# The down projections of both FFNs by seven block products over 16 of their 22 weight rows

## The chip, the cores and the metric

The kernel runs on one core of one Trainium2 chip. The metric is device time in microseconds of one execution; lower is better. The core's engines work side by side, each through its own queue in order: TensorE (PE; its weight loads are listed as PEld) multiplies, VectorE (DVE) and ScalarE (ACT) do elementwise work, GpSimd (POOL) a little of it, and SyncE (SP) issues the transfers between main memory and SBUF.

## The reference

Two layers on 512 tokens of width 1024, float32. Layer 0 mixes tokens with an RWKV-7 recurrence, layer 1 with a gated spatial unit; each is followed by a dense SwiGLU FFN with hidden width 2816, and each sub-layer sits between two RMSNorms.

```python
def _swiglu(x, w_gate, w_up, w_down):
    return (jax.nn.silu(x @ w_gate) * (x @ w_up)) @ w_down

for i in range(DEPTH):                                  # DEPTH = 2
    ...                                                 # token mixer i
    h = _rmsnorm(x, norm_gains[i, 2])
    h = _swiglu(h, ffn_w_gate[i], ffn_w_up[i], ffn_w_down[i])   # (512,1024) -> (512,1024)
    x = x + _rmsnorm(h, norm_gains[i, 3])
```

The change touches only the last product of `_swiglu`: activations of 512 tokens by 2816 times `w_down` of 2816 by 1024.

## The kernel before

**Precision.** Every float32 operand is split into two parts of type fp32r: `split` (L178) has ACT cast the tile to `hi` (L179) and DVE compute the remainder `lo` (L180). `mm3` (L201) then issues three matmuls, hi x hi, hi x lo and lo x hi (L204), into one PSUM bank. So a weight tile of 128 x 2 x 512 costs a load, a cast of 1024 columns on ACT and a remainder of 1024 columns on DVE; a row of activations costs 512 columns on each.

**Gate and up.** `ffn` (L366) makes the activations in 11 pairs of 128-row blocks. The first `PLAIN` pairs (3 in layer 0, 2 in layer 1) run directly. The others, up to pair 10, run as seven block products each, steps `p1` to `p7` (L403 to L464): two token halves of 256, two halves of the 1024 inputs, gate and up weights side by side. A step has 24 matmuls 128x128 by 128x256. Weight sums `wsum` are made by DVE (L398). PSUM banks R, Q and Z collect the products; DVE and ACT combine them (`cc<-Q` at L450, `cc<-Z` at L457, the gates at L421 and L423). Weight splits go to four rotating pairs of tiles, two in pool `wp` and two in `wx`, so that at most four are held ahead of PE.

**Down.** `out_proj` (L285) multiplies the 22 activation rows, split lazily by `down` (L503) into tiles `actw`, with `w_down`. A weight unit is two rows of 128 by one half (512) of the columns, loaded to `wraw` by SP and split by `weight` (L182). `first(0)` runs the 11 units of the first column half into four banks `acc`, one for each block of 128 tokens, unit by unit. `post0` (L316) then squares each block for its norm on ACT and multiplies it by the gain on DVE, while `first(1)` runs the second half's first eight units into four other banks. The last three units of the second half (`tail=3`) are run block by block instead, and each finished block is normalised and added to x by `post1` (L326) while PE works on the next. In layer 0 the norm of the next sub-layer follows block by block; in layer 1 each block is stored.

**Slots.** SBUF tiles of one size come from two rotating sets, 13 slots "x" and 17 slots "s". The 11 activation pairs sit in "s".

**The order.** The program is written in the order above; a scheduler then sets the order of each engine's instructions by its own model of times, and puts in the semaphores. An instruction at the head of an engine's queue holds up all behind it.

Of the kernel before, what the change touches and what calls it, by code (L numbers as in the profile page):

```python
# [7 lines left out]
F32 = mybir.dt.float32  # L8
F32R = mybir.dt.float32r
I32 = mybir.dt.int32  # L10
AF = mybir.ActivationFunctionType
ALU = mybir.AluOpType

P = 128
T = 512
# [7 lines left out]
NJ = DFF // P  # L23
# [13 lines left out]
XSLOTS = 13  # L37
LAG = 2
PLAIN = (3, 2)
DECAY = 0.5 * 0.6065306597126334  # L40


# [43 lines left out]
class Quads:  # L86
# [22 lines left out]
    def first(self):  # L109
        self.b11 = self.raw(0, 0)  # L110
        self.split(1, self.b11, "s")
        self.b21 = self.raw(1, 0)
        self.split(2, self.b21, "s")
# [17 lines left out]
class Trunk:  # L131
# [150 lines left out]
    def prenorm(self, col):  # L282
        return Norm(self, col)

    def out_proj(self, acts, wrows, nk, row, xts, store=None, tail=3, norm=None, spare=None, mid=None, after=()):  # L285


        nc = self.nc
        v = nc.vector
        gain = self.bcast_row(row)  # L290
        nu = nk // 2
        cols = [slice(0, 512), slice(512, 1024)]
        late = (1, 1) if spare else (0, tail)
        accs, f0, part = [None, None], [], []

        def mms(half, k, tt, w):
            tok = slice(tt * P, (tt + 1) * P)
            hi, lo = acts(k)
            self.mm3(accs[half][tt], (hi[:, tok], lo[:, tok]), w, k == 0, k == nk - 1)

        def unit(half, u):
            own = spare if half and u < nu - late[1] else None
# [4 lines left out]
            return [(2 * u + j, (hi[:, j, :], lo[:, j, :])) for j in range(2)]  # L307

        def first(half):
            accs[half] = self.accs(half)  # L310
            for u in range(nu - late[half]):
                for k, w in unit(half, u):
                    for tt in range(TT):
                        mms(half, k, tt, w)
# [21 lines left out]
                nc.sync.dma_start(out=store[tt * P:(tt + 1) * P, :], in_=xts[tt])  # L336

        hn_tile = lambda: self.sm.tile([P, D], F32, name="hn", tag="hn", bufs=2)
        first(0)
        if not spare:  # L340
            for tt in range(TT):
                post0(tt, hn_tile()[:, 0:512])
# [4 lines left out]
        for tt in range(TT):  # L347
# [5 lines left out]
            hn = hn_tile()  # L353
# [12 lines left out]
    def ffn(self, li, xts, norm, store=None, nxt=None, early=()):  # L366
        nc = self.nc
        early = list(early)
        v, a = nc.vector, nc.scalar
        gains = self.i["norm_gains"]  # L370
        wgu = self.gate_up(li)
        first = PLAIN[li]
        wd = self.i["ffn_w_down"][li].rearrange("(u j p) n -> u p j n", p=P, j=2)
        hT, b = norm.hT, {}
        acts, pairs, loads, seeded = [], {}, [0], []
# [123 lines left out]
                p(n)  # L499

        halves = {}

        def down(k):  # L503
            if k not in halves:
                t = halves[k] = self.slot([P, 2, T], F32R, "actw", "x" if k < XSLOTS else "s")
                self.split(t[:, 0], t[:, 1], acts[k // 2][:, k % 2])
            return halves[k][:, 0], halves[k][:, 1]

        self.out_proj(down, lambda u: wd[u], NJ, gains[li, 3], xts, store, norm=nxt)


    def load_features(self):
# [793 lines left out]
```

## Time and profile before

| | us |
|---|---|
| median of three runs | 1335.92 (1330.71 to 1341.78) |
| the profiled execution | 1336.29 |
| its span, first to last instruction | 1334.6 |
| mean granted TensorE clock | 0.981 |
| FFN 0: gate and up, about | 461 to 693 |
| FFN 0: down, about | 693 to 815 |
| FFN 1: gate and up, about | 970 to 1198 |
| FFN 1: down, about | 1198 to 1328 |

The span is the profiled execution's time less 1.7 us around it. A group's row reads: line, engine, operation, tile written <- tiles read, shapes, xcount | busy us, mean ns of one | idle time of the engine before them and what ended it. A timeline row reads: start, length, engine, line, operation, shapes, and in brackets the idle time before it with what ended it. A few records of matmuls can be missing from a trace, so a stretch may count some less than were issued.

### The profile page before, as it was taken

What the parts mean: (1) busy time and instruction counts of PE and PEld (TensorE: products, weight loads), DVE (VectorE), ACT (ScalarE), POOL (GpSimd) and SP (SyncE); (2) the same over time, 40 slices, a digit from 0 to 9 for tenths busy, and PEclk for the clock granted to TensorE, in tenths of its full rate; (3) what the DMA queues carried; (4) which work ended last, traced back from release to release, by engine and by line L of the source; (5) the groups of instructions that cost most, each with busy time, mean ns of one, the idle gap of its engine ahead of it and who ended that gap; (6) DMA issues with size and microseconds to landing.
All of it is one profiled execution on the core that took longest, in us unless ns stands there. A gap on an engine that the chain in (4) does not pass through costs nothing.

```text
span 1334.6 us, 24342 instructions
## 1 busy us (share of the span) xinstructions
PE 1281.5 (96%) x9740; PEld 1112.1 (83%) x9740; DVE 885.4 (66%) x1481; ACT 690.0 (52%) x1237; POOL 160.7 (12%) x304
## 2 busy tenths in 40 slices
PE   5999999989989899999999999999999999999998
PEld 3677799878867698999998887878888999998886
DVE  6975856567946787877874326476679878785223
ACT  7976884676533454444563315443464445464221
POOL 0000383666000012000000003020002000000000
PEclk9999999999889999999999999999989999999999
DMA  5137694322243215433423332343430443323231
GB/s 160 41 101 178 154 212 132 98 64 80 69 124 117 79 56 151 111 99 108 127 64 116 111 95 74 111 142 95 126 96 11 117 127 96 100 75 126 95 95 64
DMA packets 217202, 140.10 MB, mean 105 GB/s; under 512 B 67792, under 2 KB 193280, under 8 KB 217088
## 3 DMA queue, kind: packets, MB, share of 16 engines
q1 hardware_dynamic: 215792, 133.81, 34.9%
q0 software_dynamic: 1296, 4.72, 1.1%
q8 instruction: 77, 1.26, 0.4%
q14 instruction: 37, 0.30, 0.1%
HBM read 124.35 MB, written 14.16 MB: 104 GB/s over the span
## 4 chain that ended last, share of the span: by engine, by line
PE 66%; DVE 6%; ACT 2%; DMA 2%; issue 2%; POOL 1%; SPq 0%; DVEq 0%; ACTq 0%; POOLq 0%
PE acc L204 27%; PE Q L204 10%; PE gu L204 9%; PE R L204 7%; PE Z L204 7%; PE u L204 3%; DVE wlo L180 1%; PE gh L993 1%; DMA wraw<-in_rwkv_w_o_dram 1%; ACT hn L249 1%; ACT whi L179 1%; PE s L1240 1%; DVE wsum L400 0%; DVE tm L923 0%; ACT hT L60 0%
## 5 line engine op out<-in xcount | busy, mean ns | idle before, releaser
L180 DVE TENSOR_TENSOR wlo<-wraw,whi 128x1024 fp32r<-128x1024 f32 x117 | 144.9, 1238 | 194.8 <-ACT whi L179 194.3
L179 ACT CAST whi<-wraw 128x1024 fp32r<-128x1024 f32 x117 | 122.6, 1049 | 236.1 <-PE acc L204 143.1
L204 PE MATMUL acc<-whi,actw 128*128 128x512 f32 x704 | 220.7, 394 | 0.0
L204 PEld LDWEIGHTS acc<-whi,actw 128*128 128x128 f32 x704 | 132.2, 188 | 30.6
L204 PE MATMUL Q<-bc,whi 128*128 128x256 f32 x816 | 147.4, 281 | 2.2 <-ACT hn L444 2.2
L204 PE MATMUL acc<-wlo,actw 128*128 128x512 f32 x352 | 138.5, 394 | 0.0
L204 PEld LDWEIGHTS Q<-bc,whi 128*128 128x128 f32 x816 | 125.6, 189 | 2.7 <-ACT hn L444 2.6
L204 PE MATMUL gu<-hT,whi 128*128 128x256 f32 (+1 forms) x448 | 112.8, 344 | 2.3 <-ACT hT L60 1.2
L204 PE MATMUL Q<-bc,wlo 128*128 128x256 f32 x408 | 114.6, 281 | 0.0
L179 ACT CAST whi<-wsum 128x1024 fp32r<-128x1024 f32 x68 | 71.1, 1052 | 81.2 <-PE Q L204 24.3
L204 PE MATMUL Z<-bc,whi 128*128 128x256 f32 x544 | 99.6, 281 | 0.0
L204 PE MATMUL R<-bc,whi 128*128 128x256 f32 x544 | 98.9, 281 | 0.0
L180 DVE TENSOR_TENSOR wlo<-wsum,whi 128x1024 fp32r<-128x1024 f32 x68 | 82.2, 1221 | 22.6 <-ACT whi L179 21.6
L204 PEld LDWEIGHTS gu<-hT,whi 128*128 128x128 f32 x448 | 79.4, 199 | 12.6 <-ACT hT L60 1.9
L179 ACT CAST whi<-wq 128x1024 fp32r<-128x1024 f32 x51 | 53.5, 1049 | 68.4 <-PE gu L204 20.9
L204 PEld LDWEIGHTS Z<-bc,whi 128*128 128x128 f32 x544 | 84.0, 189 | 0.0
L204 PEld LDWEIGHTS R<-bc,whi 128*128 128x128 f32 x544 | 83.8, 188 | 0.2
L204 PE MATMUL proj<-xsp,whi 128*128 128x512 f32 x256 | 82.5, 401 | 1.3 <-ACT r L687 1.3
L180 DVE TENSOR_TENSOR wlo<-wq,whi 128x1024 fp32r<-128x1024 f32 x51 | 65.3, 1284 | 22.8 <-ACT whi L179 22.6
L204 PEld LDWEIGHTS acc<-wlo,actw 128*128 128x128 f32 x352 | 66.1, 188 | 15.1
L204 PEld LDWEIGHTS Q<-bc,wlo 128*128 128x128 f32 x408 | 77.2, 189 | 0.0
L204 PE MATMUL R<-bc,wlo 128*128 128x256 f32 x272 | 76.5, 281 | 0.0
(352 smaller groups left out, 2839.9 us busy)
## 6 DMA issues: line engine op xcount, KB each, us to landing
wraw<-in_ffn_w_down_dram SPq DMA_DIRECT2D x44, 512.0 KB, 3.7
wq<-in_ffn_w_gate_dram SPq DMA_DIRECT2D x68, 256.0 KB
wq<-in_ffn_w_up_dram SPq DMA_DIRECT2D x68, 256.0 KB, 4.3
wraw<-in_rwkv_w_rkv_dram SPq DMA_DIRECT2D x24, 512.0 KB, 5.4
wraw<-in_sgu_w_in_dram SPq DMA_DIRECT2D x16, 512.0 KB, 3.8
wraw<-in_ffn_w_gate_dram SPq DMA_DIRECT2D x10, 512.0 KB
wraw<-in_ffn_w_up_dram SPq DMA_DIRECT2D x10, 512.0 KB, 3.9
x<-in_x_dram SPq DMA_DIRECT2D x8, 512.0 KB, 3.3
```

What stands on the lines that cost most here:

```text
L179: self.nc.scalar.copy(hi, src)
L180: self.nc.vector.tensor_tensor(lo, src, hi.bitcast(F32), op=ALU.subtract)
L204: self.nc.tensor.matmul(out, l, r, start=start, stop=stop, skip_group_check=resumed)
L249: self.nc.scalar.activation(junk, src, AF.Square, accum_out=s)
L993: mm(gh[:, cc * P:(cc + 1) * P], mt[rows, cc, :], bx[rows, 0:2, cc, :], start=True, stop=True)
L1240: mm(acc[:, tt * P:(tt + 1) * P], vt[tt][:, m * P:(m + 1) * P], wsT[:, m, :], start=True, stop=True)
```

## The change

With `CROSS = (4, 4)`, each layer's down projection splits its rows: units 0 to 7 (16 rows of 128) are done by seven block products, units 8, 9 and 10 (six rows) plainly as before. `s = 4`: units 0 to 3 are the near half of the inner dimension, 4 to 7 the far half. The tokens are split into `g` (first 256) and `u` (last 256), the 1024 columns into two halves. A product `q1` to `q7` runs over four units; each unit multiplies a 256-token block of activations (split into `ablk`) by a 128 x 2 x 512 tile of weights, in 12 matmuls 128x128 by 128x512.

The eight banks have names: `R` (two banks) is the first column half of the first 256 tokens, `V` that of the last 256, `Z` and `Q` the second half of the same tokens. Each product adds into one of these pairs; where a product belongs to several outputs, ACT copies the bank to `t0` or `t1` and DVE adds the copy into another bank. `tb` and `ta` (tiles `tsum`) hold weight sums and are changed in place from step to step, `sums` (tiles `asum`) activation sums. Five of the seven products load weights, 20 loads in all, into tiles `wc` that alternate between the two buffers of `wraw` and the two of `f0`, or straight into `ta`.

The written order is p, q1, p, q5, p, q6, q2, q3, q7, q4, where each p is one plain unit's first column half into R and V. `out_proj` then gets the banks as `begun`: it does not run `first(0)`, calls `post0` for the four blocks after q4, has nothing left for `first(1)`, and runs the tail of the second half as before.

On VectorE, in layer 0, at the end of gate/up (`cc<-Q` of pair 10 up to its last product's sum `act<-cc`), before:

```order
L450 SCALAR_TENSOR_TENSOR cc<-Q,hn 128x512
L457 TENSOR_TENSOR cc<-Z,hn 128x512
L180 TENSOR_TENSOR wlo<-wraw,whi 128x1024
L180 TENSOR_TENSOR actw<-act,actw 128x512 x9
L180 TENSOR_TENSOR wlo<-wraw,whi 128x1024
L180 TENSOR_TENSOR actw<-act,actw 128x512 x2
L459 TENSOR_TENSOR act<-cc 128x2x256
```

and after, at the same place:

```order
L455 SCALAR_TENSOR_TENSOR cc<-Q,hn 128x512
L182 TENSOR_TENSOR wlo<-wc,whi 128x1024
L521 TENSOR_TENSOR tsum<-tsum,wc 128x1024
L182 TENSOR_TENSOR actw<-act,actw 128x512
L462 TENSOR_TENSOR cc<-Z,hn 128x512
L182 TENSOR_TENSOR ablk<-act,ablk 128x512 x4
L521 TENSOR_TENSOR tsum<-tsum,wc 128x1024
L577 TENSOR_TENSOR asum<-act 128x512 x2
L521 TENSOR_TENSOR asum<-act 128x512 x2
L182 TENSOR_TENSOR wlo<-wc,whi 128x1024
L182 TENSOR_TENSOR actw<-act,actw 128x512
L464 TENSOR_TENSOR act<-cc 128x2x256
```

The eleven activation splits are replaced by two of them, four block splits, two weight sums and four activation sums (L577 for q5, L521 for q7); the first `wlo<-wc` is that of q1's first unit, the second that of its second unit.

On TensorE, in layer 0, before, the change from the first column half (`acc_8091`, `acc_8092` are its last two blocks) to the second (`acc_8524` and on):

```order
L204 MATMUL acc_8091<-whi_8455,actw_8474 128x512
L204 MATMUL acc_8092<-whi_8455,actw_8474 128x512
L204 MATMUL acc_8092<-wlo_8456,actw_8474 128x512
L204 MATMUL acc_8092<-whi_8455,actw_8474 128x512
L204 MATMUL acc_8524<-whi_8530,actw_8099 128x512
L204 MATMUL acc_8524<-wlo_8531,actw_8099 128x512
```

and after, the change from q7 (`acc_8093`, `acc_8094` are Q) to q4 (`acc_8089` is V's first bank):

```order
L206 MATMUL acc_8093<-whi_8735,ablk_8732 128x512
L206 MATMUL acc_8094<-whi_8735,ablk_8732 128x512
L206 MATMUL acc_8094<-wlo_8736,ablk_8732 128x512
L206 MATMUL acc_8094<-whi_8735,ablk_8732 128x512
L206 MATMUL acc_8089<-whi_8760,ablk_8757 128x512
L206 MATMUL acc_8089<-wlo_8761,ablk_8757 128x512
```

Before, the next banks needed nothing from the last ones; now the first matmul of q4 comes after an addition of Q's copy into `acc_8089`. On VectorE that addition stands behind the one into the same Q bank:

```order
L622 TENSOR_TENSOR acc_8093<-acc_8093,hn_8107 128x512
L623 TENSOR_TENSOR acc_8089<-acc_8089,hn_8108 128x512
L622 TENSOR_TENSOR acc_8094<-acc_8094,hn_8107 128x512
L623 TENSOR_TENSOR acc_8090<-acc_8090,hn_8108 128x512
L182 TENSOR_TENSOR wlo_8818<-tsum_8106,whi_8817 128x1024
```

The last row is the weight remainder of the fourth unit of q4. The four additions stood nowhere in the program before.

```diff
@@ -37,6 +37,8 @@
 XSLOTS = 13
 LAG = 2
 PLAIN = (3, 2)
+CROSS = (4, 4)
+CROSS_ORDER = ("p1p5p62374", "p1p5p62374")
 DECAY = 0.5 * 0.6065306597126334
 
 
@@ -282,7 +284,7 @@
     def prenorm(self, col):
         return Norm(self, col)
 
-    def out_proj(self, acts, wrows, nk, row, xts, store=None, tail=3, norm=None, spare=None, mid=None, after=()):
+    def out_proj(self, acts, wrows, nk, row, xts, store=None, tail=3, norm=None, spare=None, mid=None, after=(), begun=None):
 
 
         nc = self.nc
@@ -291,12 +293,13 @@
         nu = nk // 2
         cols = [slice(0, 512), slice(512, 1024)]
         late = (1, 1) if spare else (0, tail)
-        accs, f0, part = [None, None], [], []
+        u0, accs = begun if begun else (0, [None, None])
+        f0, part = [], []
 
         def mms(half, k, tt, w):
             tok = slice(tt * P, (tt + 1) * P)
             hi, lo = acts(k)
-            self.mm3(accs[half][tt], (hi[:, tok], lo[:, tok]), w, k == 0, k == nk - 1)
+            self.mm3(accs[half][tt], (hi[:, tok], lo[:, tok]), w, k == 0, k == nk - 1, u0 > 0)
 
         def unit(half, u):
             own = spare if half and u < nu - late[1] else None
@@ -307,8 +310,9 @@
             return [(2 * u + j, (hi[:, j, :], lo[:, j, :])) for j in range(2)]
 
         def first(half):
-            accs[half] = self.accs(half)
-            for u in range(nu - late[half]):
+            if not u0:
+                accs[half] = self.accs(half)
+            for u in range(u0, nu - late[half]):
                 for k, w in unit(half, u):
                     for tt in range(TT):
                         mms(half, k, tt, w)
@@ -336,7 +340,8 @@
                 nc.sync.dma_start(out=store[tt * P:(tt + 1) * P, :], in_=xts[tt])
 
         hn_tile = lambda: self.sm.tile([P, D], F32, name="hn", tag="hn", bufs=2)
-        first(0)
+        if not begun:
+            first(0)
         if not spare:
             for tt in range(TT):
                 post0(tt, hn_tile()[:, 0:512])
@@ -499,14 +504,135 @@
                 p(n)
 
         halves = {}
+        s = CROSS[li]
 
         def down(k):
             if k not in halves:
-                t = halves[k] = self.slot([P, 2, T], F32R, "actw", "x" if k < XSLOTS else "s")
+                t = halves[k] = self.slot([P, 2, T], F32R, "actw", "x" if k - 4 * s < XSLOTS - 3 * s else "s")
                 self.split(t[:, 0], t[:, 1], acts[k // 2][:, k % 2])
             return halves[k][:, 0], halves[k][:, 1]
 
-        self.out_proj(down, lambda u: wd[u], NJ, gains[li, 3], xts, store, norm=nxt)
+        def cross():
+            accs = [self.accs(0), self.accs(1)]
+            R, V, Z, Q = accs[0][0:2], accs[0][2:4], accs[1][0:2], accs[1][2:4]
+            near = range(s)
+            act = lambda n, tok: acts[n][:, :, tok]
+            cols = (slice(0, 512), slice(512, 1024))
+            sub = lambda o, x, y: v.tensor_tensor(o, x, y, op=ALU.subtract)
+            sums = [self.slot([P, 2, 2, 256], F32, "asum", "x") for _ in near]
+            ta, tb = ([self.slot([P, 2, 512], F32, "tsum", "x") for _ in near] for _ in range(2))
+            t0, t1 = (self.sm.tile([P, 2, 512], F32, name="hn", tag="hn", bufs=2) for _ in range(2))
+            rest = list(range(2 * s, NJ // 2))
+
+            def load(n, half, t=None):
+                if t is None:
+                    pool, tag = ((self.wp, "wraw"), (self.f0p, "f0"))[loads[0] % 2]
+                    loads[0] += 1
+                    t = pool.tile([P, 2, 512], F32, name="wc", tag=tag, bufs=2)
+                nc.sync.dma_start(out=t, in_=wd[n][:, :, cols[half]])
+                return t
+
+            def parts(w):
+                self.nw += 1
+                wp = self.wx if self.nw % 2 else self.wp
+                hi, lo = (wp.tile([P, 2, 512], F32R, name=t, tag=t, bufs=2) for t in ("whi", "wlo"))
+                self.split(hi, lo, w)
+                return hi, lo
+
+            def product(ps, left, right, start=False):
+                for p in near:
+                    x, w = left(p), right(p)
+                    at = self.slot([P, 2, 2, 256], F32R, "ablk")
+                    self.split(at[:, 0], at[:, 1], x)
+                    hi, lo = parts(w)
+                    for j in range(2):
+                        for m in range(2):
+                            tok = slice(m * P, (m + 1) * P)
+                            self.mm3(ps[m], (at[:, 0, j, tok], at[:, 1, j, tok]), (hi[:, j], lo[:, j]),
+                                     start and p == 0 and j == 0, p == s - 1 and j == 1, True)
+
+            def straight():
+                n = rest.pop(0)
+                hi, lo = parts(load(n, 0))
+                for j in range(2):
+                    ah, al = down(2 * n + j)
+                    for m, q in enumerate(R + V):
+                        tok = slice(m * P, (m + 1) * P)
+                        self.mm3(q, (ah[:, tok], al[:, tok]), (hi[:, j], lo[:, j]), n == 2 * s and j == 0,
+                                 not rest and j == 1, True)
+
+            def q1():
+                def w(p):
+                    t = load(p, 0)
+                    load(p, 1, ta[p])
+                    sub(tb[p], ta[p], t)
+                    return t
+                product(Q, lambda p: act(p, g), w, True)
+                for m in range(2):
+                    a.copy(t1[:, m], Q[m])
+                    v.tensor_tensor(R[m], R[m], t1[:, m], op=ALU.add)
+
+            def q5():
+                def x(p):
+                    v.tensor_tensor(sums[p][:, 0], act(p, u), act(s + p, u), op=ALU.add)
+                    return sums[p][:, 0]
+                product(Z, x, lambda p: tb[p], True)
+                for m in range(2):
+                    a.copy(t0[:, m], Z[m])
+
+            def q6():
+                def x(p):
+                    sub(sums[p][:, 0], sums[p][:, 0], act(p, g))
+                    return sums[p][:, 0]
+
+                def w(p):
+                    sub(tb[p], load(s + p, 1), tb[p])
+                    return tb[p]
+                product(Q, x, w)
+                for m in range(2):
+                    a.copy(t1[:, m], Q[m])
+
+            def q2():
+                def w(p):
+                    t = load(s + p, 0)
+                    sub(tb[p], t, tb[p])
+                    return t
+                product(R, lambda p: act(s + p, g), w)
+
+            def q3():
+                def x(p):
+                    sub(sums[p][:, 0], act(s + p, g), sums[p][:, 0])
+                    return sums[p][:, 0]
+
+                def w(p):
+                    t = load(s + p, 1)
+                    sub(ta[p], t, ta[p])
+                    return t
+                product(Z, x, w)
+                for m in range(2):
+                    v.tensor_tensor(Z[m], Z[m], t1[:, m], op=ALU.add)
+
+            def q7():
+                def x(p):
+                    sub(sums[p][:, 1], act(p, g), act(p, u))
+                    return sums[p][:, 1]
+                product(Q, x, lambda p: ta[p])
+                for m in range(2):
+                    a.copy(t1[:, m], Q[m])
+                    v.tensor_tensor(Q[m], Q[m], t0[:, m], op=ALU.add)
+                    v.tensor_tensor(V[m], V[m], t1[:, m], op=ALU.add)
+
+            def q4():
+                product(V, lambda p: act(s + p, u), lambda p: tb[p])
+
+            steps = {"1": q1, "2": q2, "3": q3, "4": q4, "5": q5, "6": q6, "7": q7, "p": straight}
+            for step in CROSS_ORDER[li]:
+                steps[step]()
+            return 2 * s, accs
+
+        begun = cross() if s else None
+
+        self.out_proj(down, lambda u: wd[u], NJ, gains[li, 3], xts, store, norm=nxt, begun=begun)
 
 
     def load_features(self):
```

## The prediction

> **What bounds the kernel now.** I read the page's busy times first, then its forty slices, then the stretches of the two FFNs, and last the chain of waits in the down projections.
>
> ```profile
> span 1334.6 us, 24342 instructions
> PE 1281.5 (96%) x9740; PEld 1112.1 (83%) x9740; DVE 885.4 (66%) x1481; ACT 690.0 (52%) x1237; POOL 160.7 (12%) x304
> PE   5999999989989899999999999999999999999998
> DVE  6975856567946787877874326476679878785223
> ```
>
> TensorE is near full nearly everywhere; VectorE changes by stage. The stretches below are, for each layer, gate/up and then down (busy us and instruction count of PE, PEld, DVE, ACT, POOL; then clock and DMA).
>
> ```profile
> 461.00:693.00 232.00, 229.65 (x1721) 219.64 (x1722) 185.31 (x247) 117.31 (x182) 15.86 (x12) 0.99 0.37 105
> 693.00:815.00 122.00, 122.00 (x545) 99.61 (x545) 44.94 (x66) 37.87 (x56) 3.85 (x3) 1.00 0.32 100
> 970.00:1198.00 228.00, 224.07 (x1762) 217.84 (x1763) 186.39 (x251) 118.29 (x187) 10.93 (x9) 0.99 0.32 91
> 1198.00:1328.00 130.00, 130.00 (x597) 106.83 (x595) 49.48 (x76) 38.42 (x59) 0.00 (x0) 1.00 0.28 90
> ```
>
> In both down stages PE is busy for the whole stretch and DVE for 37 to 38% of it. In gate/up, which already uses seven products, DVE is busy 80 to 82% and PE still idles only 2 to 4 us. So down is bound by PE alone. The chain gives the price of its matmuls (start, length, what):
>
> ```profile
> 693.57 4.20 PE acc L204 x18
> 697.77 2.88 PE Q L204 x24
> 1203.23 4.34 PE acc L204 x19
> 1207.57 2.80 PE Q L204 x24
> 1210.37 117.75 PE acc L204 x509
> ```
>
> Layer 1's 19 + 509 = 528 matmuls take 4.34 + 117.75 = 122.1 us, 0.231 us each. The 24 Q matmuls are gate/up's last product (step 4 of pair 10), which stands between the first down matmuls.
>
> **What PE saves.** Before, a layer's down issues 22 rows x 4 token blocks x 2 halves x 3 = 528 matmuls. After: 7 products x 4 units x 12 = 336, plus three plain units, 72 in the first half and 72 in the second, 480. The shape stays 128x128 by 128x512. 48 fewer x 0.231 = 11.1 us per layer, 22.2 in all, if PE is never held.
>
> The Trainium skill (TensorE: Matmul & The Clock Gate, Back-to-back issue gap) gives 131 ns per 512-column matmul sustained. By it 96 matmuls would be 12.6 us; the trace's 231 ns disagrees and decides.
>
> **What VectorE and ScalarE pay.** The group rows give durations (count | busy, mean ns), the timelines the pace of back-to-back work.
>
> ```profile
> L180 DVE TENSOR_TENSOR wlo<-wraw,whi 128x1024 fp32r<-128x1024 f32 x22 | 26.9, 1223 | 64.3 <-ACT whi L179 64.2
> L179 ACT CAST whi<-wraw 128x1024 fp32r<-128x1024 f32 x22 | 23.1, 1048 | 70.4 <-PE acc L204 63.7 <-PE Q L204 3.5 <-DMA wraw<-in_ffn_w_down_dram 3.0
> L179 ACT CAST actw<-act 128x512 fp32r<-128x512 f32 x15 | 8.4, 616 | 0.7 <-DVE act L459 0.7
> 674.36 1.22 DVE L400 TENSOR_TENSOR wsum<-wsum,wq 128x1024 f32<-128x1024 f32 x1
> 675.49 0.68 DVE L459 TENSOR_TENSOR act<-cc 128x512 f32<-128x512 f32 x1
> 695.35 5.50 DVE L180 TENSOR_TENSOR actw<-act,actw 128x512 fp32r<-128x512 f32 x9
> ```
>
> Queued closely, a 1024-column DVE operation takes 1.13 us (674.36 to 675.49; I use 1.14) and a 512-column one 5.50 / 9 = 0.61 (I use 0.60). Per layer, DVE before: 22 x 1.14 + 22 x 0.60 = 38.3. After: 34 weight remainders (38.8), 16 weight sums (18.2), 34 activation remainders (20.4), 16 activation sums (9.6) and 8 additions in PSUM (4.8, priced as 512 columns): 91.8. That is 53.5 more, all in a stage of about 111 us. ACT goes from 22 x 1.05 + 22 x 0.62 = 36.7 to 34 x 1.05 + 34 x 0.62 + 8 copies x 0.59 = 61.5, below PE throughout.
>
> ```profile
> wraw<-in_ffn_w_down_dram SPq DMA_DIRECT2D x44, 512.0 KB, 3.7
> 686.49 0.59 ACT L444 COPY hn<-Q 128x512 f32<-128x512 f32 x1
> ```
>
> Loads go from 22 to 26 per layer on SP's queue, 13.6 MB in 111 us: 123 GB/s, where the gate/up stretch had 105. Each lands in 3.7 us, and the four rotating tiles give four units, 4 x 12 x 0.231 = 11.1 us, so I cost them at nothing. With half of that cover gone, a tile's round (landing 3.7, sum 1.14, cast 1.05, remainder 1.14, together 7.0) stands against 5.5, 1.5 us lost in every two units.
>
> **Can DVE feed PE?** A unit of a product is 12 x 0.231 = 2.78 us of PE. Its DVE price: q1 and q2 2.88 (sum, two remainders), q5 and q7 2.34, q6 and q3 3.48, q4 1.74; a plain unit 2.34 against 5.54. Weighed over the stage DVE is just cheap enough; what counts is the start. The order puts 4 weight sums, 8 activation sums, 4 activation remainders and 4 weight remainders ahead of pair 10's last gate, in place of nine activation splits.
>
> ```profile
> L204 PE MATMUL acc<-whi,actw x704: 387/395/475, 693.4 to 1327.7; 128*128 128x512 f32 x176
> 692.79 0.69 DVE L450 SCALAR_TENSOR_TENSOR cc<-Q,hn 128x512 f32<-128x512 f32 x1 [2.34 <-PE Q L204]
> 672.44 1.23 DVE L180 TENSOR_TENSOR wlo<-wsum,whi 128x1024 fp32r<-128x1024 f32 x1 [0.28 <-ACT whi L179]
> 676.75 1.23 DVE L180 TENSOR_TENSOR wlo<-wsum,whi 128x1024 fp32r<-128x1024 f32 x1 [0.57 <-ACT whi L179]
> 1202.43 0.69 DVE L450 SCALAR_TENSOR_TENSOR cc<-Q,hn 128x512 f32<-128x512 f32 x1 [2.33 <-PE Q L204]
> ```
>
> Layer 0, from `cc<-Q` at 692.8 down DVE's order to the weight remainder of q1's second unit: eleven 512-column operations (6.6), four of 1024 (4.6) and 0.3 of waiting for ACT make 11.5 (704.3). PE asks for it after 18 plain matmuls, the 2.81 us Q product and 14 of q1: 693.4 + 32 x 0.231 + 2.8 = 703.6. Held 0.7. The third unit's comes 4.7 later (709.0); PE asks at 704.3 + 13 x 0.231 = 707.3. Held 1.7. In layer 1 DVE has one weight sum fewer there (10.3 from 1202.4, then 4.7: 1212.7 and 1217.4) and PE has 24 plain matmuls ahead and four before the third unit's remainder (1203.2 + 38 x 0.231 + 2.8 = 1214.8, and 14 x 0.231 later 1218.0): nothing.
>
> From there to q7, DVE's order read in the same way is 2.7 to 6 us ahead of each request, if DVE never idles. It does idle 0.28 to 0.57 when it reaches a remainder before ACT's cast, as the two rows show. Of 28 units some will hit this: between 0 (lead covers all) and 28 x 2 x 0.3 = 17 less the 2.7 lead, 14 us. Most sums and casts stand a unit or more ahead in the order, so I take an estimate near the low end, 2 us per layer.
>
> **q7 to q4.** q4 adds into V, which waits for ACT's copy of Q, DVE's addition into Q and only then DVE's addition into V; every q4 matmul and, behind it, all of the tail stand behind that on PE's queue. On the kernel's last block the trace shows such a hand-over:
>
> ```profile
> 1328.15 0.60 ACT L249 ACTIVATE hn<-acc 128x512 f32<-128x512 f32 x1 [3.17 <-PE acc L204]
> 1328.87 0.69 DVE L329 TENSOR_TENSOR hn<-acc,gain 128x512 f32<-128x512 f32 x1 [1.40 <-ACT hn L249]
> PE Q L204 <- ACT hn L444: 1.1, 1, 1.1
> ```
>
> From the start of Q's last matmul: 0.45 until ACT has it (1327.7 to 1328.15), copy 0.59, additions 0.60 and 0.69, 0.08 between: 2.4, less the four matmul places that it and the other block still fill, 0.9: held 1.5 per layer. Bounds: 1.1 (the one wait of PE for an ACT copy above) and 2.4.
>
> **Tail.** What the kernel's third block cost DVE, first and last row, and the first half's gain products:
>
> ```profile
> 1324.68 0.69 DVE L329 TENSOR_TENSOR hn<-acc,gain 128x512 f32<-128x512 f32 x1 [1.41 <-ACT hn L249]
> 1326.72 0.75 DVE L332 SCALAR_TENSOR_TENSOR x<-hn,ry,x 128x512 f32<-128x512 f32 x1
> L321 DVE TENSOR_TENSOR f<-acc,gain 128x512 f32<-128x512 f32 x4 | 2.7, 685 | 1.9 <-ACT hn L249 1.9
> ```
>
> The gain products (2.7) and the squares move into the tail of 72 matmuls, 16.6 us, which hides them; without that cover they cost 2.7. The blocks now end 34, 29, 17 and 0 matmuls before the end of PE (7.9, 6.7, 3.9, 0 us). Each takes DVE 2.8 us (1324.68 to 1327.47), from 0.7 after its end: the fourth finds DVE 0.5 late. 0.5 per layer, between 0 and 2.8.
>
> **Clock.** Does a held PE cost clock too?
>
> ```profile
> 826.41 0.79 PE L204 MATMUL acc<-whi,hT 128*128 128x512 f32 x1 [2.02 <-ACT hT L60]
> 825.00:830.00 5.00, 3.59 (x9) 2.87 (x10) 4.83 (x22) 5.00 (x18) 0.58 (x1) 0.66 0.57 191
> 478.60:815.00 336.40, 335.09 (x2149) 303.12 (x2149) 214.36 (x249) 142.34 (x193) 17.36 (x11) 1.00 0.35 104
> ```
>
> After 2.02 us of idle PE the clock is 0.66 over 5 us, that is 3.4 us at half speed, 1.7 lost. After the 1.1 us wait, inside the long stretch, it stays 1.00. My 1.7 hold is nearest the first, the 1.5 ones nearest the second: one drop, 1.7, in layer 0; bounds 0 and 3 x 1.7. The Trainium skill (TensorE: Matmul & The Clock Gate, HAM oscillation) warns only of gaps over about 3.4 us. By it there is no drop and the sum gains 1.7; the 2.02 us row disagrees, so I keep it.
>
> **Sum.** Layer 0: 11.1 - 2.4 - 2 - 1.5 - 0.5 - 1.7 = 3.0. Layer 1: 11.1 - 2 - 1.5 - 0.5 = 7.1. Together 10.1. The profiled execution took 1336.29, so 1326.2; that run lies 0.4 above the median 1335.92, so 1325.8 on it. I say 1326.
>
> **Rivals.**
> - *PE is hardly held*: gate/up shows PE full with DVE at 80%, and from pair 10's last gate to q4 DVE is asked for 70 us (91.8 less 18 done ahead and 3.4 in the tail) in 390 x 0.231 = 90, 78%. Holds under 3 us per layer, no drop: 1314 to 1322. Against: the start of layer 0, and q7 to q4. Chance 0.27.
> - *DVE sets the pace by hand-offs*: the 14 us above in place of 2 in each layer: 11.1 - 14 leaves 3 lost per layer, up to 1343; decides once hand-off waits exceed the 2.7 lead. Against: DVE's sums stand ahead. 1332 to 1343, chance 0.22.
> - *Slower: a unit's chain runs in series*: sum 1.22, cast 1.05, remainder 1.23 and two hand-overs of 0.3 make 4.1 us against 2.78; if in the 16 units with a weight sum nothing is done ahead (loads late, or casts stuck behind ACT's copies out of PSUM, which wait for a product's end), 16 x 1.3 - 11.1 = 10 per layer lost: 1356. It decides when the lead falls under one unit. Against: four split buffers and the order. Chance 0.11.
>
> **Chances.** The forecast (1322 to 1332) has 0.40. A measurement of this kernel tells about 1%, 13.4 us, from no change: faster than 1322.6 is the first rival's 0.27 and 0.07 of the forecast, 0.34; slower 0.11; the rest 0.55. The range leaves out the slow case and a little of both ends: 1314 to 1341.
>
> **What would show it.** Right: 480 down matmuls per layer; DVE 75 to 85% busy from the first plain unit to q4; PE waits on weight remainders in layer 0's q1 and none in layer 1's; one wait of 1.1 to 2.4 us on V before q4 per layer; down 3 to 7 us shorter. Wrong: PE waits on remainders all through q6, q2 and q3 (the hand-off or series case), waits on loads, half clock in both stages, or a changed gate/up time.

## The result, and the profile after

The changed kernel takes 1324.54 us (median of 6 runs, 1323.67 to 1329.32); the kernel before, run beside it on the same chip, 1334.78 (6 runs). The ratio is 0.9925, 95% interval 0.990 to 0.995: 10.2 us less. The forecast was 1326.

The page of the changed kernel, busy times and slices as before:

```profile
span 1322.0 us, 24413 instructions
PE 1260.2 (95%) x9644; PEld 1093.2 (83%) x9644; DVE 990.8 (75%) x1609; ACT 739.6 (56%) x1303; POOL 161.3 (12%) x304
PE   5999999989989899999999998999999999999998
DVE  7975756477956687878779967476679877888985
```

PE has 96 matmuls fewer. DVE is 105 us busier (990.8 against 885.4), and its two low stretches, 4 3 2 at slices 22 to 24 and 5 2 2 3 at the end, have become 9 9 6 and 8 9 8 5. The groups that write `acc` in the two down stages (tile view; min/mean/max ns, first to last):

```profile
L206 PE MATMUL acc<-whi,actw x192: 388/393/400, 692.7 to 1315.1; 128*128 128x512 f32 x192
L206 PE MATMUL acc<-wlo,actw x96: 387/395/400, 693.0 to 1314.9; 128*128 128x512 f32 x96
L206 PE MATMUL acc<-whi,ablk x448: 387/394/504, 699.8 to 1298.3; 128*128 128x512 f32 x150
L206 PE MATMUL acc<-wlo,ablk x224: 388/394/496, 700.0 to 1298.1; 128*128 128x512 f32 x112
```

192 + 96 + 448 + 224 = 960, 480 per layer, as counted. The stretches of the two block-product phases, columns as in the prediction:

```profile
705.00:712.00 7.00, 5.55 (x25) 4.18 (x24) 7.00 (x11) 3.71 (x5) 0.00 (x0) 1.00 0.50 162
712.00:780.00 68.00, 68.00 (x294) 54.94 (x293) 62.30 (x73) 38.74 (x51) 1.45 (x2) 1.00 0.33 104
780.00:785.00 5.00, 3.60 (x16) 2.62 (x15) 4.58 (x7) 3.47 (x7) 0.00 (x0) 1.00 0.02 5
1199.00:1285.00 86.00, 86.00 (x387) 70.27 (x386) 81.90 (x100) 50.57 (x69) 0.00 (x0) 1.00 0.34 106
```

PE never idles in the middle of either stage, though DVE is busy for 92% and 95% of it. It idles at three places of the two stages and at the hand-over behind layer 0's (timeline rows of PE; idle time before the row, with what ended it, in brackets). Of these four, only behind the hand-over does the clock fall (last row, a stretch of 5 us):

```profile
707.69 0.50 PE L206 MATMUL acc<-wlo,ablk 128*128 128x512 f32 x1 [1.45 <-DVE wlo L182]
782.61 0.47 PE L206 MATMUL acc<-whi,ablk 128*128 128x512 f32 x1 [1.40 <-DVE acc L623]
1287.29 0.50 PE L206 MATMUL acc<-whi,ablk 128*128 128x512 f32 x1 [1.31 <-DVE acc L623]
816.30 1.22 PE L206 MATMUL acc<-whi,hT 128*128 128x512 f32 x2 [3.44 <-DVE hT L64]
815.00:820.00 5.00, 3.70 (x10) 2.90 (x11) 5.00 (x14) 3.99 (x10) 2.50 (x2) 0.66 0.59 204
```

The first is a weight remainder of layer 0's q1, the next two are q4 waiting for the addition into V, the fourth is the SGU's first products waiting for the normed last block. Where the time went, worked out from the first and last matmul of each stage in each profile, good to 0.1 (three experiments beside it; down ends with its last matmul, in the kernel before at 819.6, behind the stretch that the prediction reads):

| stage, us | before | after | q2 late | pinned | all three |
|---|---|---|---|---|---|
| to layer 0's gate/up | 461.2 | 460.0 | 461.6 | 459.0 | 458.8 |
| gate/up 0 | 232.2 | 232.7 | 232.9 | 231.4 | 232.5 |
| down 0 | 126.2 | 118.0 | 117.2 | 118.0 | 115.2 |
| hand-over, to the SGU's u | 51.9 | 54.2 | 48.8 | 54.0 | 48.6 |
| rest of the SGU | 103.1 | 103.2 | 102.5 | 103.2 | 102.5 |
| gate/up 1 | 228.5 | 231.4 | 231.3 | 227.8 | 230.2 |
| down 1 | 125.0 | 116.0 | 114.4 | 116.0 | 114.2 |
| end | 6.5 | 6.5 | 6.5 | 6.5 | 6.5 |
| span | 1334.6 | 1322.0 | 1315.2 | 1315.9 | 1308.5 |

The down stages gave 8.2 and 9.0. The hand-over gave back 2.3 and layer 1's gate/up, which the change does not touch, 2.9. Of the 8.2 and of the 2.3, 0.8 only crossed the border between the two stages: eight transposes for the next norm, which stood in the tail and now stand behind it. Before, then after:

```profile
814.38 1.04 PE L279 MATMUL ptr<-ident,x 128*128 128x128 f32 x8
810.70 1.04 PE L281 MATMUL ptr<-ident,x 128*128 128x128 f32 x8
```

The last down matmul starts at 819.2 before and at 810.3 after, and until the next matmul the eight take 0.8. So the real loss at the hand-over is 1.5, nearly all of it the longer wait (3.44 for 2.02), and layer 0's down gave 7.4. The columns q2 late, pinned and all three belong to experiments below. The first row covers work that no edit touches, and it still runs from 457.4 to 462.0 over the twelve profiles of this study; a single profile's total is good to no more than that, and its stages say more.

The 2.9 is one wait. VectorE in layer 1's gate/up, first the kernel before (two rows), then the changed kernel, and last its PE:

```profile
1037.52 1.21 DVE L180 TENSOR_TENSOR bc<-tsum,bc 128x1024 fp32r<-128x1024 f32 x1
1038.65 2.35 DVE L400 TENSOR_TENSOR wsum<-wq 128x1024 f32<-128x1024 f32 x2
1029.58 0.41 DVE L426 TENSOR_TENSOR act<-sg,R 128x256 f32<-128x256 f32 x1
1032.62 1.23 DVE L405 TENSOR_TENSOR wsum<-wq 128x1024 f32<-128x1024 f32 x1 [2.62 <-DMA wq<-in_ffn_w_up_dram]
1034.90 1.22 DVE L182 TENSOR_TENSOR bc<-tsum,bc 128x1024 fp32r<-128x1024 f32 x1
1036.17 0.39 PE L206 MATMUL Z<-bc,whi 128*128 128x256 f32 x1 [2.95 <-DVE bc L182]
```

DVE stands 2.62 us at a weight sum of the next pair, whose load has just been issued; the remainder `bc` that PE needs now is queued behind it. Before, the scheduler had put `bc` ahead of that sum. The order of a stage that nobody edited had changed: on DVE one sum had moved up past two rows.

### The profile page after: what moved, and what is told of

The parts are those of the page before. It is cut to its first block, busy times and chain, and to the rows that moved or that the text cites. A ratio compares the mean times of both kernels' runs of the same rounds, so it can differ in the third digit from the quotient of the medians.

```text
span 1322.0 us, 24413 instructions
## 1 busy us (share of the span) xinstructions
PE 1260.2 (95%) x9644; PEld 1093.2 (83%) x9644; DVE 990.8 (75%) x1609; ACT 739.6 (56%) x1303; POOL 161.3 (12%) x304
## 4 chain that ended last, share of the span: by engine, by line
PE 65%; DVE 9%; ACT 2%; DMA 1%; issue 1%; SPq 0%; DVEq 0%; ACTq 0%
PE acc L206 25%; PE Q L206 10%; PE Z L206 7%; PE gu L206 7%; PE R L206 6%; PE u L206 3%; DVE wlo L182 1%; PE gh L1119 1%; DVE wsum L405 1%; PE lm L1004 1%; DVE x L336 1%; PE Yp L1161 1%; PE mp L1112 1%; DMA wraw<-in_rwkv_w_o_dram 1%; PE s L1366 1%
## 5 line engine op out<-in xcount | busy, mean ns | idle before, releaser
L182 DVE TENSOR_TENSOR wlo<-wraw,whi 128x1024 fp32r<-128x1024 f32 x79 | 98.7, 1249 | 72.2 <-ACT whi L181 71.8
L206 PE MATMUL acc<-whi,ablk 128*128 128x512 f32 x448 | 141.6, 395 | 2.7 <-DVE acc L623 2.7
L181 ACT CAST whi<-wraw 128x1024 fp32r<-128x1024 f32 x79 | 82.8, 1049 | 103.2 <-PE acc L206 31.5
L206 PEld LDWEIGHTS acc<-whi,ablk 128*128 128x128 f32 x448 | 84.1, 188 | 23.3 <-ACT hn L621 1.8
L206 PE MATMUL acc<-wlo,ablk 128*128 128x512 f32 x224 | 88.5, 395 | 1.4 <-DVE wlo L182 1.4
L206 PE MATMUL Z<-bc,wlo 128*128 128x256 f32 x272 | 76.3, 281 | 0.0
```

The source lines that it names most:

```text
L181: self.nc.scalar.copy(hi, src)
L182: self.nc.vector.tensor_tensor(lo, src, hi.bitcast(F32), op=ALU.subtract)
L206: self.nc.tensor.matmul(out, l, r, start=start, stop=stop, skip_group_check=resumed)
```

## The experiments

Times are medians, and ratios go against runs of the kernel before on the same chip (its medians there were 1333.07 to 1334.92). The changed kernel's 1324.54 was measured earlier, beside 1334.78, and its own runs lie up to 5.7 apart.

### One layer at a time

```diff
-CROSS = (4, 4)
+CROSS = (4, 0)        # layer 0 alone;  (0, 4): layer 1 alone
```

> Only layer 0's down projection by block products; layer 1's as before. Both theories take the median of before, 1334.8, as the base. Theory A (the matmuls saved come through less two short holds, and the rest is lost outside the down stage): PE's down stage is 8.3 us shorter, the hand-over to the spatial unit 2.4 longer, layer 0's gate/up 0.5 longer, and layer 1's gate/up 2.9 longer by a new wait on a split of the block sums' input, because VectorE's order at its start is the changed one here too. Together 2.5 us faster, 1332.3. Theory B (both layers give about the same, some 5 us of 10, the rest eaten by VectorE in the down stages): 5 us faster, 1329.8.

> Only layer 1's down projection by block products; layer 0's as before. Theory A: the down stage is 9.0 us shorter, nothing follows it, and VectorE's order at the start of layer 1's gate/up is that of before, so the 2.9 wait is not there: 9 us faster, 1325.8, nearly all that the whole change gave. Theory B: 5 us faster, 1329.8.

Layer 0 alone: 1334.95, ratio 1.0001 (0.9986 to 1.0015). Layer 1 alone: 1326.21, ratio 0.9943 (0.9925 to 0.9961). Within the intervals all of the gain is layer 1's, and layer 1 alone comes close to the first theory's 1325.8. Layer 0 alone gave neither theory's figure. Yet its down is 8.2 shorter (126.2 to 118.0), as the first theory had it. The hand-over takes 3.7 more and not 2.4, with a longer spell of half clock (last section), and gate/up 1 takes 6.0 more, not 2.9: the same wait, and this time the clock halves behind it. PE's row and the stretches, layer 0 alone, then the same stretch of the changed kernel:

```profile
1036.84 0.58 PE L206 MATMUL Z<-bc,whi 128*128 128x256 f32 x1 [2.87 <-DVE bc L182]
1035.00:1040.00 5.00, 3.16 (x15) 3.16 (x16) 5.00 (x6) 2.48 (x3) 0.00 (x0) 0.60 0.00 0
1040.00:1045.00 5.00, 5.00 (x33) 5.00 (x33) 2.97 (x3) 1.53 (x2) 0.00 (x0) 0.71 0.38 111
```

```profile
1035.00:1040.00 5.00, 3.83 (x32) 3.83 (x33) 4.97 (x6) 3.44 (x5) 0.00 (x0) 1.00 0.01 3
```

5 x 0.40 + 5 x 0.29 = 3.4 us short of full clock, so a spell of 6.8 us at half clock behind 2.87 us of idle PE; behind 2.95 us at the same place the changed kernel's profile shows none. With layer 1 alone changed, gate/up 1 takes 228.8 and the wait does not exist: it is layer 0's change that reorders it.

### The wait in layer 1's gate/up

```diff
+            with (self.tc.issue_after(quads.rem5.ins) if li == 1 and n == first + 1 else ExitStack()):
                 o["s"] = wsum(o["a21"], o["a22"])
```

and the same around the sum in `p7`; `rem5` is the remainder `bc<-tsum`.

> Changed kernel, with one thing pinned in layer 1's gate/up: the first two weight sums of the second pair (whose two loads land late) may not be issued on VectorE ahead of the remainder bc<-tsum, which they stood ahead of in the changed kernel and behind in the kernel before. Theory A (the 2.9 us wait of PE in layer 1's gate/up is only the place of that remainder behind a sum that waits 2.62 us for its load): the wait goes, gate/up takes 228.5 again, 1324.5 - 2.9 = 1321.6. Rival (the loads come late whatever stands ahead of them, and the wait moves to the product that reads their sum): 231.4 and 1324.5 stay, with a wait of about 2.9 one product later.

1321.32, ratio 0.9892 (0.9873 to 0.9912), with 1321.6 forecast. Gate/up 1 takes 227.8. What PE waits for in it and in the SGU ahead (total us, times, longest):

```profile
PE ptr L282 <- DVE hT L64: 2.9, 2, 2.5
PE Q L207 <- ACT hn L451: 1.1, 1, 1.1
PE gu L207 <- ACT hT L62: 0.7, 1, 0.7
```

The wait for `bc` is gone, and none of its size has taken its place. The first theory stands for the changed kernel: two instructions in the wrong order, 3 us.

### From q7 to q4, and q2 later

```diff
-CROSS_ORDER = ("p1p5p62374", "p1p5p62374")
+CROSS_ORDER = ("p1p5p63724", "p1p5p63724")
```

> The steps in the order p, q1, p, q5, p, q6, q3, q7, q2, q4: q2, which adds into the first 256 tokens' banks, stands between q7 and q4. Theory A: the two holds before q4 (1.40 and 1.31 us) go, since the copy and additions run beside q2's 48 matmuls; VectorE keeps up with q6 and q3 in a row from its lead, so 2.7 us faster than the change, 1321.8. Rival (VectorE is the pace in the middle of the stage): eight units at 3.48 us of VectorE against 2.78 of PE in a row ask 5.6 us more than PE gives; with a lead of 2.7 to 3, PE is held 2 to 3 us on weight remainders in q3, and the time stays at 1324.5.

1316.87, ratio 0.9879 (0.986 to 0.9898): 7.7 less than the changed kernel, where 2.7 was expected. PE's waits from layer 0's down to the SGU's first products, all there are:

```profile
PE acc L206 <- DVE wlo L182: 1.4, 1, 1.4
PE acc L206 <- DVE hT L64: 0.5, 1, 0.5
```

With q2's 48 matmuls between q7 and q4 the holds ahead of q4 are gone in both layers, as expected. The surplus is in the hand-over, 48.8 for 54.2: the wait for `hT` is 0.5 and not 3.44, and the clock stays at 1.00. In PE's order the tail's blocks now end nearly one after the other, as in the kernel before. The wait is 2.9 of the 5.4, the spell of half clock that is missing 1.7, and the eight transposes, which stand in the tail again, 0.8. Gate/up 1, at 231.3, still loses 2.9 to a wait, but to another one, some 17 us later in the stage, on a `wlo` that stands on DVE behind a sum and its late load.

```diff
-CROSS_ORDER = ("p1p5p62374", "p1p5p62374")
+CROSS_ORDER = ("p1p56237p4", "p1p56237p4")
```

> Changed kernel, with the third plain unit's first column half between q7 and q4 in place of between q5 and q6. Theory A (its 24 matmuls, 5.5 us, cover the hand-over from q7 to q4): no hold of 1.3 to 1.4 ahead of q4 in either layer; the last two blocks end 18 matmuls apart, and the hand-over to the SGU loses 0 to 2.3: 1324.5 - 2.7 - (0 to 2.3) = 1319.5 to 1321.8. Rival (that unit gave VectorE 5.54 - 2.34 = 3.2 us of lead ahead of q6, whose units cost it 3.48 against 2.78; without it PE waits on remainders in q6 and q3): 1 to 3 us per layer lost there, 1322 to 1327.

1320.94, ratio 0.9925 (0.9897 to 0.9953, against 1333.07 of the kernel before): inside the first theory's numbers, but not for its reason. PE's waits from layer 0's first product to q4, and the three rows behind them:

```profile
PE acc L206 <- DVE wlo L182: 2.3, 2, 1.4
PE acc L206 <- DVE acc L623: 1.3, 1, 1.3
708.64 0.50 PE L206 MATMUL acc<-wlo,ablk 128*128 128x512 f32 x1 [1.44 <-DVE wlo L182]
739.32 0.50 PE L206 MATMUL acc<-wlo,ablk 128*128 128x512 f32 x1 [0.83 <-DVE wlo L182]
781.74 0.50 PE L206 MATMUL acc<-whi,actw 128*128 128x512 f32 x1 [1.33 <-DVE acc L623]
```

The hold ahead of q4 (1.3) is still there. In PE's order the scheduler had moved half of the plain unit's matmuls, those into R, ahead between the products, and only the 12 into V stand at q4. These add into the bank that q4 waits for, so the wait (last row) is now that of the first of them: they could not have covered it. A new hold on a remainder, 0.83, came without the unit's lead. Down takes 119.9 and 117.9, 1.9 more than in the changed kernel each, which are the rival's numbers (in layer 0, 0.8 of it are the eight transposes, back in the tail); the hand-over takes 51.7, 2.5 less. These stages add up to more than the changed kernel, and the profiled execution, 1325.61, agrees; the median is 3.6 below it. Why the other three executions (1320.4 to 1321.3, at a mean clock of 0.983 to 0.988 against the profile's 0.982) were faster stays open; a spell of half clock more or less (last section) would be part of it.

### The start of q1

```diff
-                    sub(sums[p][:, 1], act(p, g), act(p, u))
-                    return sums[p][:, 1]
+                    sub(sums[p][:, 0], act(p, g), act(p, u))
+                    return sums[p][:, 0]
```

> Changed kernel, with q7's activation sums written where q5, q6 and q3 had theirs, so that they cannot be made ahead of q1. Theory A (the 1.45 us hold on the third weight remainder of layer 0's q1 is the 4 x 0.6 us of those sums ahead of it): the hold goes, 1324.5 - 1.4 = 1323.1, nothing else moves. Rival (q7 then waits for a sum, a cast and a remainder that come only after q3's last split): q1 gains 1.4 and each q7 loses 1 to 2, 1324.5 to 1327.

1320.64, ratio 0.9895 (0.9881 to 0.991). PE's waits from 690 to 800, all there are:

```profile
PE acc L206 <- DVE acc L623: 1.4, 1, 1.4
```

The hold on q1's third remainder is gone, and q7 does not wait. Down 0 takes 116.0, 2.0 less (1.45 of it the hold). The total fell by 3.9, more than that, but the interval overlaps the changed kernel's (0.990 to 0.995), and in its profile 3.8 of the gain lie ahead of down 0, where nothing was edited. Gate/up 1 takes 234.8 there, with the later wait on a `wlo` (2.6) and half clock behind it.

### How near the bound is VectorE

```diff
                     self.split(at[:, 0], at[:, 1], x)
+                    sub(at[:, 1], x, at[:, 0].bitcast(F32))
```

> Changed kernel, with the remainder of every product unit's activation block computed twice (28 units per layer, one more VectorE instruction of 512 columns each, 0.60 us, 16.8 us per layer; the values are the same). Theory A (VectorE, 92 to 94% busy in the middle of down, is the next bound with 5 to 7 us of idle left there): down grows by 8 to 11 us per layer, 1324.5 + 16 to 22 = 1340 to 1346, and PE waits on remainders in q6, q3 and q2. Rival (half of what reads as busy is slack that PE does not see, its lead of a unit or more covers it): 0 to 4 us per layer, 1325 to 1332.

1347.65, ratio 1.0091 (1.0065 to 1.0117): 23 us more than the changed kernel, slower than before. Down grew by 12.7 and 14.0, beyond even the first theory. PE's waits of layer 0's down, the middle of that stage, and the stretches in and behind the 3.3 and the 3.8:

```profile
PE acc L206 <- DVE acc L624: 3.8, 1, 3.8
PE acc L206 <- DVE ablk L521: 3.3, 1, 3.3
PE acc L206 <- DVE wlo L182: 2.2, 4, 0.8
712.00:780.00 68.00, 65.72 (x279) 51.71 (x278) 68.00 (x85) 38.04 (x51) 1.45 (x2) 1.00 0.34 108
700.00:705.00 5.00, 2.58 (x6) 2.12 (x7) 5.00 (x9) 0.62 (x1) 0.00 (x0) 0.61 0.35 105
705.00:710.00 5.00, 5.00 (x17) 3.94 (x17) 5.00 (x8) 2.28 (x4) 0.00 (x0) 0.71 0.33 105
790.00:795.00 5.00, 3.92 (x9) 3.18 (x10) 4.70 (x11) 1.34 (x4) 0.00 (x0) 0.50 0.01 3
```

DVE now never idles in the middle of the stage. The two long holds stand in q1 and ahead of q4; on the remainders, where the first theory had the whole loss, PE waits only 2.2. The holds come to 9.3, which is 6.5 more than the 2.85 of the changed kernel. The half clock behind the first long one costs 5 x 0.39 + 5 x 0.29 = 3.4, that behind the second as much, and the two cover the rest of the 12.7. Layer 1 is held 9.9, 3.2 of it on casts of ACT. So the changed kernel's margin on DVE is below the 0.60 us per unit that was added, and past it a held PE loses clock as well.

### The hand-over

The edit, shortened:

```diff
             for half in range(2):
                 for k, w in ends[half]:
-                    mms(half, k, tt, w)
+                    mms(half, k, tt, w, u0 > 0)     # pins the first of each three matmuls on PE
```

> Changed kernel, with the first matmul of each of the four groups of every token block's tail (18 matmuls, three plain units' second column half) pinned behind all PE work written ahead of it, so that the blocks end 18 matmuls apart as in the kernel before, and not bunched. Theory A (the hand-over from layer 0's down to the SGU is longer because the blocks end close together and VectorE, which takes 2.8 us for each, finishes the last ones late): from the end of layer 0's down to the u projection 51.9 again and not 54.2, 1324.5 - 2.3 = 1322.2; the end of the kernel and layer 1's gate/up stay. Rival (the tail's weight remainders come late, and PE interleaves blocks for that reason; pinned it waits for them at the first block): 0 to 3 us lost in the tail, 1324.5 to 1326.

The hand-over takes 51.9 again, and the wait is before's:

```profile
PE acc L206 <- ACT hT L62: 2.1, 1, 2.1
```

So the longer wait, 1.4 of the 2.3, comes of the bunched ends of the tail's blocks; the transposes, back in the tail, are 0.8 of the 2.3 and also 0.8 of the 1.1 that down 0 takes more in this profile. The two stages together give 1.2. The time is 1325.0 (1321.54 to 1327.92, ratio 0.9933, 0.9907 to 0.9959) and not 1322.2: gate/up 1 takes 234.5 in the profile, with the later wait on a `wlo` (2.8) and half clock behind it. By the total this run is inconclusive.

The second edit, shortened:

```diff
+    own1 = lambda n, sh, t: self.slot(sh, t, n, "x")    # the second half's weights are split into "x" slots
-            own = spare if half and u < nu - late[1] else None
+            own = spare if half and u < nu - late[1] else own1
```

> The weights of the tail (second column half, last three units) are split into slots of the sums, free by then, and not into the four rotating pairs, so that they stand ready and TensorE's order in the tail is nearly block by block (7+4+11+14, 18, 18 matmuls). Theory A (the longer hand-over in layer 0 comes from blocks that finish bunched): PE's wait after the tail falls from 3.4 to about 2 us, 2.4 us faster than the change in layer 0 and nothing in layer 1: 1322.1. Rival (the first half's squares and gain products, which now stand in the tail on ScalarE and VectorE, make the hand-over late whatever the order of the blocks): the wait stays at 3.4, 1324.5.

1328.78, ratio 0.9956 (0.9934 to 0.9977): worse than the changed kernel, by neither theory. Down became 1.4 and 1.6 shorter, because the holds ahead of q4 are gone: in PE's order 42 and 53 of the tail's 72 plain matmuls now stand ahead of q4. But the hand-over stayed at 54.8, though its longest wait fell to 1.7, gate/up 1 took 233.1, and the end of the kernel 11.8 in place of 6.5. There q4, which finishes V, ends 19 matmuls before PE's last and not 72; ACT idles 13.3 us until it can square these blocks, and the norms of all four blocks end behind PE's last matmul. An edit that frees tiles frees the scheduler too.

### All three together

The order with q2 late, q7's sums in place, and the two pinned sums.

> The order 1 5 6 3 7 2 4 of the products, q7's activation sums in place, and the two pinned sums, all three together. Theory A (the three act in different places and add up): 1316.9 - 1.4 - 2.9 = 1312.6. Rival (a second load that VectorE waits for, 3.2 us in the profile of the order 1 5 6 3 7 2 4, holds PE 2.9 us in layer 1's gate/up as well, and q7 with sums in place waits): 1315 to 1318.

1310.22 (1308.5 to 1310.98), ratio 0.9813 (0.9798 to 0.9828): 24.7 us below the kernel before and 14.3 below the changed one. The middles of the two down stages:

```profile
712.00:780.00 68.00, 68.00 (x295) 55.08 (x294) 65.33 (x79) 41.00 (x57) 1.44 (x2) 1.00 0.30 93
1190.00:1275.00 85.00, 85.00 (x381) 69.41 (x380) 82.39 (x102) 49.64 (x69) 0.00 (x0) 1.00 0.32 100
```

PE waits nowhere in either down stage, with DVE busy for 96 to 97% of these stretches. Down takes 115.2 and 114.2: 11.0 and 10.8 less than before, which is the 11.1 that 48 matmuls are worth. The two terms that were to go besides (1.4 of q1's hold, 2.9 of gate/up 1) gave 2.0 and 1.1 against the order with q2 late. In gate/up 1 PE's listed waits fell by 3.7, more than was asked, but half clock at the start of the stage, which the profile with q2 late lacks, took much of it back (last section). Against the kernel before, gate/up 1 at 230.2 keeps 1.7, of which PE's list shows 0.6 on a remainder. So the three edits act in different places, as the first theory had it; that the total is 2.4 below its 1312.6 is no gain of theirs as far as the profile shows, since 2.8 of its difference from q2 late lie ahead of layer 0's gate/up.

## Why the forecast was right, and where its steps were not

The time is right, and partly by errors that cancelled. In the profiled executions 1336.29 became 1323.67, 12.6 less, against a sum of 10.1; 1.2 of it lies in the first 460 us.

**What PE saves, 11.1 per layer.** Right: 480 matmuls per layer, and the kernel without holds saves 11.0 and 10.8. Layer 0's down: 11.1 - 1.45 - 1.40 = 8.25, measured 8.2, but without the transposes that left the stage 7.4. Layer 1's: 11.1 - 1.31 = 9.8, measured 9.0. So both fall short by about 0.8. Taken without the listed waits, a matmul of these stages took 0.233 us, against 0.232 before and with all three edits, which over 480 is the 0.8; why is not shown.

**The start of q1, 0.7 + 1.7 in layer 0, none in layer 1.** Right in kind, one term too many. The third unit's remainder held PE 1.45. The second's ended 11.3 after `cc<-Q`, as counted (11.5), but `cc<-Q` stood 1.1 ahead of the first down matmul (691.6 and 692.7) and not 0.6 (692.8 and 693.4).

**Hand-offs, 2 per layer.** This step failed: no PE wait in either layer from q1's fourth unit to q4. The sums and casts stood far enough ahead, as the text said before it charged 2 all the same. Down was to be 3 to 7 us shorter with it; it was 8.2 and 9.0.

**Loads, at nothing.** Right: PE waits for none in either stage. (Four of the seven products load weights, not five; the 20 loads are right.)

**DVE 75 to 85% busy.** Wrong: 92 to 95%. The step failed in its denominator: the 70 us of DVE's work were counted from pair 10's last gate, the 390 matmuls from the start of the stage, and 24 of these are the shorter Q matmuls, which take 2.9 us together. The stretch from the stage's start to q4:

```profile
692.00:783.00 91.00, 88.15 (x394) 71.23 (x393) 84.88 (x104) 52.82 (x73) 1.45 (x2) 1.00 0.34 107
```

In it DVE is busy for 84.9 us, 93% of 91; from the gate, at 707.6, to q4, at 782.6, there are 75 us for the 70. With the right figure the case that DVE sets the pace would have looked likelier than 0.22; it needed only the 0.60 us per unit of the doubled remainder.

**q7 to q4, 1.5 per layer.** Right: 1.40 and 1.31, and with q2 in between nothing.

**Clock, 1.7 in layer 0.** It did not come: after 1.45 and 1.40 the stretches 705 to 712 and 780 to 785 show 1.00. Longer holds in down do, as the doubled remainder showed.

**Tail, 0.5 per layer.** Mis-sized in layer 0 and needless in layer 1. The block ends were read rightly, but the 2.8 us per block of DVE were reckoned to the end of the tail and not on to the next stage, where the last blocks' norm is followed by transposes and splits: 1.4 there (the wait of 3.44 for 2.02, and 2.06 again with the blocks pinned). Layer 1's end is 6.5 in both.

**Not in the sum: 2.9 in layer 1's gate/up.** The text named a changed gate/up time as a sign of being wrong, and it came. The order of that stage was not read.

So within the down stages the first rival was nearer (holds under 3 us per layer, no drop), and the time came to the forecast because more than 4 us were lost outside them, 1.5 at the hand-over and 2.9 in gate/up 1. That was luck. Of the other rivals, the pace set by hand-offs and the series chain, no wait was seen.

## What to carry to other kernels

Where a scheduler sets the order, an edit in one stage can swap two instructions in another, so compare the orders of the stages that weren't touched too, and look for an instruction that PE needs now behind one whose load has just been issued. When work moves from a full engine to one that becomes 95% full, count the second engine's work and the first one's time from the same instant. And give a product that must wait for a copy and an addition another product to stand behind: in this kernel that order was worth more than the hold itself, because it changed the order of the tail as well.

## What had not been expected of the hardware

How long PE idles does not decide alone whether its clock halves, and for how long. The wait for `hT` at the hand-over is 3.44 us in the changed kernel, with layer 0 alone changed and with the pinned sums. Layer 0 alone:

```profile
815.13 1.22 PE L206 MATMUL acc<-whi,hT 128*128 128x512 f32 x2 [3.44 <-DVE hT L64]
810.00:815.00 5.00, 1.69 (x14) 1.25 (x11) 4.93 (x9) 3.97 (x15) 2.64 (x3) 0.92 0.55 173
815.00:820.00 5.00, 4.87 (x14) 3.90 (x15) 5.00 (x14) 3.35 (x9) 2.87 (x2) 0.50 0.42 142
820.00:825.00 5.00, 5.00 (x23) 4.09 (x23) 3.22 (x16) 4.04 (x14) 0.00 (x0) 0.90 0.34 105
```

and with the pinned sums:

```profile
814.02 0.73 PE L207 MATMUL acc<-whi,hT 128*128 128x512 f32 x2 [3.44 <-DVE hT L64]
815.00:820.00 5.00, 5.00 (x27) 4.06 (x27) 4.89 (x12) 3.65 (x11) 2.38 (x1) 1.00 0.44 127
```

The first is a spell of 2 x 5 x (0.08 + 0.50 + 0.10) = 6.8 us at half clock, the second none; the changed kernel's 0.66 over 5 us was one of 3.4, and so was that behind the 2.02 us in the kernel before. The Trainium skill (TensorE: Matmul & The Clock Gate, Part 1: The HAM clock gate) says that the clock follows activity in a free-running window of about 3.4 us. Spells of 3.4 and 6.8 us, and outcomes that differ behind one and the same wait, agree with it; its rule against gaps over about 3.4 us (HAM oscillation) does not mark the bound here, since 2.02 us cost a spell and 3.44 once did not. That the position of the window decides is argued, not shown. The start of layer 1's gate/up says the same. PE waits 2.5 us for `hT` just ahead of it in all twelve profiles; a spell of 6.8 us follows in ten of them, one of 3.4 us with the pinned sums, and none with q2 late. The first row is from q2 late, where this wait ends at 961.2, the second from all three edits, where it ends at 955.8:

```profile
960.00:965.00 5.00, 2.49 (x15) 1.81 (x16) 5.00 (x19) 5.00 (x18) 0.00 (x0) 1.00 0.95 272
960.00:965.00 5.00, 5.00 (x28) 5.00 (x28) 5.00 (x21) 3.49 (x14) 0.00 (x0) 0.56 0.51 130
```

For a forecast of this kernel it means that a wait of 2 to 3.5 us carries a clock term that is drawn anew, 0 to 3.4 us short of full clock.

With PE at 100% and DVE at 96 to 97% of the same stretch, no wait appeared in the kernel with all three edits; a second engine that full had been taken for a possible bound.
